# Turned FFN input projection: all 512-column products of a contraction half, then all 256-column ones

## The chip, the cores and the metric

The kernel runs on one core of a Trainium2 chip, in one launch. The core has five engines with queues of their own: TensorE (PE: matmuls, with its weight loads listed as PEld), VectorE (DVE), ScalarE (ACT), GpSimd (POOL) and SyncE (SP, which issues most of the DMAs). TensorE adds its products up in PSUM, of which the kernel uses eight banks of 128 partitions x 512 floats; everything else lies in SBUF. The metric is the device time of one execution in microseconds, as the median over several runs.

## The reference

Two layers of a streaming encoder on 256 tokens of width 1024, all in 32-bit floats. Each layer has a half-step FFN, a mixer (differential attention beside an mLSTM) and a second half-step FFN, each between a norm before and a norm after. The change lies in the FFN alone, which runs four times (two layers, two each):

```python
D_MODEL, SEQ, DEPTH, D_FF = 1024, 256, 2, 2816

def _swiglu(h, w_in, w_out):
    gate, up = jnp.split(h @ w_in, 2, axis=-1)
    return (jax.nn.silu(gate) * up) @ w_out

h = _swiglu(_rmsnorm(x, g[0]), ffn_w_in[l, 0], ffn_w_out[l, 0])
x = x + 0.5 * _rmsnorm(h, g[1])
```

So per FFN 256 tokens are multiplied with a 1024 x 5632 matrix, gate and up are combined, and the result is multiplied with a 2816 x 1024 matrix.

## The kernel before

**Three products for one.** TensorE multiplies in a reduced format (float32r). To keep precision, each operand is split into a high part, rounded to that format, and a low part, what is left of it. A product is then high x high + high x low + low x high. The weights are split on the chip: `begin_piece` (line 276) loads a piece of 128 x 2048 floats (1 MB) by a DMA on SyncE into a tile `wr`; for each half of it ScalarE makes the high part `wh` (line 287) and VectorE the low part `wl` (line 288). The split takes 324 instructions of each kind.

**Chunks.** The 2816 hidden columns are cut into 11 chunks of 256 (`NC_FF`). A chunk needs three pieces of weights: two of the input matrix, one for each half of the contraction of 1024 (`kh` 0 and 1), and one of the output matrix. The loop over chunks is in `ffn` (line 588, loop from line 661). The first two chunks of a pass are computed token-major, `in_piece` with `mm3` (lines 400 to 402).

**Turned chunks.** From chunk 2 (`TURN`) on, nine chunks to a pass, the projection is turned: the weights are the stationary operand and the tokens move, so that the hidden block comes out with hidden columns on partitions. `in_turned` (line 603) computes a chunk for one half of the contraction. There are four blocks of 128 output columns, two for gate and up (`i`) times two (`j`), each with a PSUM bank of its own: `banks[0]` are two banks with the tag `pin`, `banks[1]` two with the tag `ptr`. For each block and each of four slices of the contraction (`k`) there are two matmuls:

- line 610: the high part of the weights, against `both`, where the high parts of all 256 tokens stand beside their low parts: 512 columns, high x high in the left half of the bank and high x low in the right half;
- line 613: the low part of the weights, against the high parts of the tokens alone: 256 columns, added to the left half of the bank.

The order before is block by block: four of line 610, four of line 613, then the next block. It is called twice, for `kh` 0 and 1, and both halves add up in the same banks.

**Evacuation.** `ffn_turned` and `ffn_block` (lines 575 and 561) take two banks per `j`: ScalarE copies the right half of a bank to SBUF (line 567), VectorE adds the left half to it (line 568; then the bank is free) and scales by token (line 569); ScalarE takes the SiLU of the gate (line 571, recorded at line 265), VectorE multiplies by the up part (line 572). `ffn_hilo` splits the hidden block for the output product (lines 545 and 546).

**Output product.** `out_part` (line 597) multiplies a hidden block with the output weights: 24 matmuls of 512 columns for a chunk, in four banks `bk`. It runs two chunks behind (`DEFER`). So the ordinary chunk on TensorE is: 32 matmuls of `kh` 0, 32 of `kh` 1, 24 of the output product of an earlier chunk. The last three output products of a pass come at its end, the first token half first (lines 689 to 697).

**What sets the order.** The engines' queues are in order. A planner places the instructions by priority and by readiness in a plan of its own; so TensorE's order can differ from the order in the source, except for the end of a pass (from "ending") and the first chunk, where the source's order is kept. Tiles and banks come from pools with a fixed number of buffers, and a write waits until the buffer's last reader is done.

Of the kernel before, what the change touches and what calls it, by code (L numbers as in the profile page):

```python
# [24 lines left out]
P = 128  # L25
D = 1024
S = 256
NT = S // P
# [102 lines left out]
class _Trunk:  # L131
# [456 lines left out]
    def ffn(self, pre, gi_post):  # L588
# [13 lines left out]

        def in_turned(banks, w, kh, both):

            for j in range(2):
                for i in range(2):
                    c = slice(i * 256 + j * P, i * 256 + j * P + P)
                    b = banks[j][i]
                    for k in range(4):
                        self.nc.tensor.matmul(b, self.cols(w, k)[0][:, c], both[:, k].rearrange("p i t -> p (i t)"),  # L610
                                              start=kh == 0 and k == 0, stop=False, skip_group_check=True)
                    for k in range(4):
                        self.nc.tensor.matmul(b[:, 0:NT * P], self.cols(w, k)[1][:, c], both[:, k, 0:NT].rearrange("p i t -> p (i t)"),  # L613
                                              start=False, stop=kh == 1 and k == 3, skip_group_check=True)

        po, pend = None, []
        if not xT:
# [43 lines left out]
        for c in range(begin, NC_FF):  # L661
            ws = [self.piece(), self.piece()]
            pend.append((c - 1, h, self.piece()))
            if c == 3:
                g = self.load_gpost(gi_post)
                yield "middle"
            if c < TURN:
                pins = [self.bank_pin() for _ in range(NT)]
                for kh in range(2):
                    for t in range(NT):  # L670
                        in_piece(t, kh, pins[t], ws[kh])
                h = [self.ffn_evac(pins[t], r[t]) for t in range(NT)]
            else:
                if c == TURN:
                    rows, both = self.token_scales(r), list(self.both)
                banks = [[self.bank_pin() for _ in range(2)], [self.bank_tr() for _ in range(2)]]
                for kh in range(2):
                    in_turned(banks, ws[kh], kh, both[kh])
                if c == NC_FF - 1:
                    break  # L680
                h = self.ffn_turned(banks, rows, c > NC_FF - DEFER - 1)
            if len(pend) == DEFER - 1 or po is None:
                if po is None:
                    po = [[self.bank_bk() for _ in range(2)] for _ in range(NT)]
                cc, hc, wo = pend.pop(0)
                for t in range(NT):
                    out_part(cc, t, hc, wo)
# [567 lines left out]
```

## Time and profile before

| | us |
|---|---|
| runs shown (three) | 977.34, 977.02, 977.38; median 977.34 |
| the profiled execution, time | 978.05 |
| its span, first to last instruction | 976.3 |
| TensorE busy in it | 968.3 |
| TensorE weight loads | 817.2 |
| VectorE busy | 710.5 |
| ScalarE busy | 567.5 |

The span is shorter than the execution's time, since what lies ahead of the first instruction and behind the last one isn't in it. Busy time counts the time in which an engine had an instruction under way; for TensorE, whose matmuls overlap, it says little of how well the array is used, and the distance from one start to the next says more. In the views below, "out<-in" are the program's tiles with buffer numbers left out (`pin<-both,wh`: into a bank `pin`, from `both` and `wh`), "128*128 128x512" is the stationary operand and the moving operand of a matmul, "x4" the number of instructions that were merged into the row, and a bracket tells the idle time ahead of a row and what ended it.

### The profile page before, as it was taken

How to read it: one execution, taken by the hardware profiler on the slowest of the kernel's cores; microseconds unless marked ns; L12 is line 12 of the kernel's file. 1: busy time of each engine (PE TensorE's matmuls, PEld its weight loads, DVE VectorE, ACT ScalarE, POOL GpSimd, SP SyncE). 2: the span in 40 equal slices, each digit the busy share in tenths (PEclk: the TensorE clock that was granted, in tenths of full speed). 3: DMA queues.
4: the chain of work that ended last, by engine and by line, in shares of the span. 5: the costliest groups of instructions: out<-in, count | busy, mean ns of one | idle time of the engine just before them, and what ended most of it. 6: DMA issues, size and time to landing. Idle time of an engine off the chain costs nothing.

```text
span 976.3 us, 13528 instructions
## 1 busy us (share of the span) xinstructions
PE 968.3 (99%) x5067; PEld 817.2 (84%) x5067; DVE 710.5 (73%) x1177; ACT 567.5 (58%) x1041; POOL 29.0 (3%) x55
## 2 busy tenths in 40 slices
PE   9999999999999999999999999999999999999997
PEld 6888888888788888888888888888888888888886
DVE  6787676689867677667687767676997687776764
ACT  7665555477856565455475545454778475555541
POOL 2000000000010000000000000000001000000000
PEclk9999999999999999999999999999999999999999
DMA  8864545336352844564356455443454256644511
GB/s 305 335 224 167 198 170 205 134 130 232 115 193 95 315 170 175 186 238 177 133 203 241 149 206 216 175 170 116 171 211 173 87 208 239 215 176 177 198 61 44
DMA packets 27648, 178.94 MB, mean 183 GB/s; under 512 B 3034, under 2 KB 4186, under 8 KB 6846
## 3 DMA queue, kind: packets, MB, share of 16 engines
q1 hardware_dynamic: 27006, 177.46, 49.5%
q8 instruction: 40, 0.66, 0.3%
q10 hardware_dynamic: 576, 0.61, 0.2%
q14 instruction: 26, 0.21, 0.1%
HBM read 177.01 MB, written 1.05 MB: 182 GB/s over the span
## 4 chain that ended last, share of the span: by engine, by line
PE 99%; DMA 1%; DVE 0%; SPq 0%; ACT 0%; POOLq 0%; issue 0%; DVEq 0%; ACTq 0%
PE ptr L610 14%; PE pin L610 14%; PE bk L402 10%; PE bk L401 10%; PE bk L400 10%; PE pin L400 7%; PE pin L402 7%; PE pin L401 7%; PE ptr L613 7%; PE pin L613 7%; PE ptr L877 1%; PE ptr L426 1%; PE bk L1092 1%; PE bk L1130 1%; DMA x<-in_x_dram 1%; PE bk L378 0%
## 5 line engine op out<-in xcount | busy, mean ns | idle before, releaser
L288 DVE TENSOR_TENSOR wl<-wr,wh 128x1024 fp32r<-128x1024 f32 x324 | 388.6, 1222 | 127.2 <-ACT wh L287 125.2
L287 ACT ACTIVATE wh<-wr 128x1024 fp32r<-128x1024 f32 x324 | 332.2, 1053 | 121.1 <-PE ptr L610 55.9
L610 PE MATMUL pin<-both,wh 128*128 128x512 f32 x576 | 157.3, 394 | 0.0
L610 PE MATMUL ptr<-both,wh 128*128 128x512 f32 x576 | 157.0, 394 | 0.0
L401 PE MATMUL bk<-wl,hh 128*128 128x512 f32 x352 | 137.6, 391 | 0.0
L400 PE MATMUL bk<-wh,hh 128*128 128x512 f32 x352 | 137.4, 390 | 0.0
L402 PE MATMUL bk<-wh,hl 128*128 128x512 f32 x352 | 136.8, 391 | 0.0
L400 PE MATMUL pin<-wh,both 128*128 128x512 f32 x304 | 122.4, 404 | 0.0
L401 PE MATMUL pin<-wl,both 128*128 128x512 f32 x304 | 119.1, 392 | 0.0
L402 PE MATMUL pin<-wh,both 128*128 128x512 f32 x304 | 118.8, 391 | 0.0
L610 PEld LDWEIGHTS pin<-both,wh 128*128 128x128 f32 x576 | 100.6, 189 | 14.9
L610 PEld LDWEIGHTS ptr<-both,wh 128*128 128x128 f32 x576 | 98.8, 189 | 13.8
L613 PEld LDWEIGHTS ptr<-both,wl 128*128 128x128 f32 x576 | 88.3, 189 | 12.2
L613 PEld LDWEIGHTS pin<-both,wl 128*128 128x128 f32 x576 | 88.2, 189 | 11.7
L613 PE MATMUL pin<-both,wl 128*128 128x256 f32 x576 | 92.4, 281 | 0.0
L613 PE MATMUL ptr<-both,wl 128*128 128x256 f32 x576 | 91.6, 281 | 0.0
L545 ACT ACTIVATE hh<-su 128x256 fp32r<-128x256 f32 (+1 forms) x96 | 32.1, 355 | 95.4 <-PE bk L401 79.1
L402 PEld LDWEIGHTS bk<-wh,hl 128*128 128x128 f32 x352 | 66.1, 188 | 14.0
L401 PEld LDWEIGHTS bk<-wl,hh 128*128 128x128 f32 x352 | 66.1, 188 | 12.9
L400 PEld LDWEIGHTS bk<-wh,hh 128*128 128x128 f32 x352 | 66.1, 188 | 12.8
L402 PEld LDWEIGHTS pin<-wh,both 128*128 128x128 f32 x304 | 57.1, 188 | 12.4
L400 PEld LDWEIGHTS pin<-wh,both 128*128 128x128 f32 x304 | 57.2, 188 | 11.8 <-issue 0.7
(202 smaller groups left out, 978.4 us busy)
## 6 DMA issues: line engine op xcount, KB each, us to landing
wr<-in_w_dram SPq DMA_DIRECT2D x162, 1024.0 KB, 4.8
gpost<-in_gpost_dram SPq DMA_DIRECT2D x6, 512.0 KB, 5.7
wr<-in_w_dram SPq DMA_DIRECT2D x2, 512.0 KB, 6.9
wr<-in_w_dram SPq DMA_DIRECT2D x3, 256.0 KB, 5.1
x<-in_x_dram SPq DMA_DIRECT2D x3, 256.0 KB, 5.7
out_dram<-x SPq DMA_DIRECT2D x2, 256.0 KB, 2.4
x<-in_x_dram SPq DMA_DIRECT2D x2, 128.0 KB, 2.8
wr<-in_w_dram ACTq DMA_DIRECT2D x1, 256.0 KB, 3.7
```

What stands on the lines that cost most here:

```text
L287: ia = nc.scalar.activation(hi, raw[:, j], AF.Copy)
L288: iv = nc.vector.tensor_tensor(lo, raw[:, j], hi.bitcast(F32), op=ALU.subtract)
L400: mm(ps, xh, wh, start=start, stop=False)
L401: mm(ps, xh, wl, start=False, stop=False)
L402: mm(ps, xl, wh, start=False, stop=stop)
L426: nc.tensor.transpose(ptr[:, k, :], x[:, (4 * hf + k) * P:(4 * hf + k + 1) * P], self.ident)
L545: self.nc.scalar.activation(hh, h, AF.Copy)
L610: self.nc.tensor.matmul(b, self.cols(w, k)[0][:, c], both[:, k].rearrange("p i t -> p (i t)"), start=kh == 0 and k == 0, stop=False, skip_ ...
L613: self.nc.tensor.matmul(b[:, 0:NT * P], self.cols(w, k)[1][:, c], both[:, k, 0:NT].rearrange("p i t -> p (i t)"), start=False, stop=kh == ...
L877: self.T(ptr[:, b, :], a[:, b * P:(b + 1) * P], self.tr.ident)
L1092: self.mm(pcs[c][:, h, :], self.qkT[0][rows, h0 + h, t * P:(t + 1) * P], self.qkT[1][rows, h0 + h, 0:nk], start=True, stop=True)
L1130: self.mm(po[:, h, :], self.aT[t][:, kt, h, :], self.vd[:, kt, h * P:(h + 1) * P], start=kt == 0, stop=kt == t)
```

## The change

Within each half of the contraction, `in_turned` goes over the four blocks twice: first all sixteen products of 512 columns (four blocks times four slices, line 610 before), then all sixteen of 256 columns (line 613 before). The blocks, their banks, the operands, the number of matmuls, and which of them starts and which ends the sum in a bank stay the same.

```diff
         def in_turned(banks, w, kh, both):
 
-            for j in range(2):
-                for i in range(2):
-                    c = slice(i * 256 + j * P, i * 256 + j * P + P)
-                    b = banks[j][i]
-                    for k in range(4):
-                        self.nc.tensor.matmul(b, self.cols(w, k)[0][:, c], both[:, k].rearrange("p i t -> p (i t)"),
-                                              start=kh == 0 and k == 0, stop=False, skip_group_check=True)
-                    for k in range(4):
-                        self.nc.tensor.matmul(b[:, 0:NT * P], self.cols(w, k)[1][:, c], both[:, k, 0:NT].rearrange("p i t -> p (i t)"),
-                                              start=False, stop=kh == 1 and k == 3, skip_group_check=True)
+            blocks = [(banks[j][i], slice(i * 256 + j * P, i * 256 + j * P + P)) for j in range(2) for i in range(2)]
+            for b, c in blocks:
+                for k in range(4):
+                    self.nc.tensor.matmul(b, self.cols(w, k)[0][:, c], both[:, k].rearrange("p i t -> p (i t)"),
+                                          start=kh == 0 and k == 0, stop=False, skip_group_check=True)
+            for b, c in blocks:
+                for k in range(4):
+                    self.nc.tensor.matmul(b[:, 0:NT * P], self.cols(w, k)[1][:, c], both[:, k, 0:NT].rearrange("p i t -> p (i t)"),
+                                          start=False, stop=kh == 1 and k == 3, skip_group_check=True)
```

## The prediction

> **What bounds the kernel now.** I read the page first: its span, busy times, granted clock and the chain that ended last.
>
> ```profile
> span 976.3 us, 13528 instructions
> PE 968.3 (99%) x5067; PEld 817.2 (84%) x5067; DVE 710.5 (73%) x1177; ACT 567.5 (58%) x1041; POOL 29.0 (3%) x55
> PEclk9999999999999999999999999999999999999999
> PE 99%; DMA 1%; DVE 0%; SPq 0%; ACT 0%; POOLq 0%; issue 0%; DVEq 0%; ACTq 0%
> ```
>
> TensorE is 99% of the chain, its clock is at full speed in every slice, and no other engine holds more than 1% of the chain. A busy TensorE proves little by itself, since the ends of matmuls are modelled, so I looked next at what TensorE waits for (the list of waits, TensorE alone).
>
> ```profile
> PE bk L389 <- PEq L1245: 0.8, 1, 0.8
> PE ptr L348 <- DMA x<-in_x_dram: 0.5, 1, 0.5
> PE bk L376 <- ACT wh L366: 0.4, 1, 0.4
> ```
>
> That is the whole list: 1.7 us, all of it in the opening stage (lines 348, 376 and 389). Behind it TensorE never waits for weights, for a bank or for an evacuation. The time of this kernel is therefore the sum of the distances from one matmul's start to the next, and the change can act in two ways only: it alters those distances, or it makes a wait where there is none. How many matmuls are concerned is in the costliest groups (line, engine, operation, shapes, count, then busy time, mean duration in ns, idle time before).
>
> ```profile
> L288 DVE TENSOR_TENSOR wl<-wr,wh 128x1024 fp32r<-128x1024 f32 x324 | 388.6, 1222 | 127.2 <-ACT wh L287 125.2
> L287 ACT ACTIVATE wh<-wr 128x1024 fp32r<-128x1024 f32 x324 | 332.2, 1053 | 121.1 <-PE ptr L610 55.9
> L610 PE MATMUL pin<-both,wh 128*128 128x512 f32 x576 | 157.3, 394 | 0.0
> L610 PE MATMUL ptr<-both,wh 128*128 128x512 f32 x576 | 157.0, 394 | 0.0
> L613 PE MATMUL pin<-both,wl 128*128 128x256 f32 x576 | 92.4, 281 | 0.0
> L613 PE MATMUL ptr<-both,wl 128*128 128x256 f32 x576 | 91.6, 281 | 0.0
> ```
>
> There are 1152 products of 512 columns and 1152 of 256, 32 of each to a chunk, so 36 turned chunks (9 in each of four FFN passes). Their durations of 394 and 281 ns overlap, so they are no prices. The price is the distance of starts, and the timeline gives it. This is one ordinary chunk, with the last ten output matmuls ahead of it (start, length, engine, line, shapes, count):
>
> ```profile
> 112.63 0.39 PE L402 MATMUL bk<-wh,hl 128*128 128x512 f32 x1
> ...
> 114.90 1.07 PE L610 MATMUL pin<-both,wh 128*128 128x512 f32 x4
> 115.81 0.64 PE L613 MATMUL pin<-both,wl 128*128 128x256 f32 x4
> 116.28 1.09 PE L610 MATMUL pin<-both,wh 128*128 128x512 f32 x4
> 117.21 0.63 PE L613 MATMUL pin<-both,wl 128*128 128x256 f32 x4
> 117.68 1.09 PE L610 MATMUL ptr<-both,wh 128*128 128x512 f32 x4
> ...
> 126.10 0.40 PE L400 MATMUL bk<-wh,hh 128*128 128x512 f32 x1
> ```
>
> The ten output matmuls, all of 512 columns, take 114.90 - 112.63 = 2.27 us, 0.227 each. The first four turned products of 512 columns, right behind them, take 0.91, still 0.2275 each. After the first four of 256 columns (0.47), the next four of 512 take 0.93, 0.2325 each. The same instruction costs about 5 ns more after a run of short ones. The whole chunk takes 126.10 - 114.90 = 11.20 us.
>
> **The change part by part.** No instruction is added or removed: the same 2304 matmuls with the same weight loads, the same banks, the same DMAs. What changes is the order within each half of the contraction: four long runs of four and four short ones become one of sixteen each. So I need the price of long runs. The planner has made a few in the first chunks of a pass, where it took blocks out of turn:
>
> ```profile
> 339.48 1.09 PE L610 MATMUL pin<-both,wh 128*128 128x512 f32 x4
> 340.41 1.07 PE L610 MATMUL ptr<-both,wh 128*128 128x512 f32 x4
> 341.31 0.64 PE L613 MATMUL ptr<-both,wl 128*128 128x256 f32 x4
> ...
> 345.52 0.63 PE L613 MATMUL ptr<-both,wl 128*128 128x256 f32 x4
> 345.99 0.64 PE L613 MATMUL pin<-both,wl 128*128 128x256 f32 x4
> 346.47 1.09 PE L610 MATMUL pin<-both,wh 128*128 128x512 f32 x4
> ...
> 353.00 0.28 PE L613 MATMUL ptr<-both,wl 128*128 128x256 f32 x1
> 353.11 1.09 PE L610 MATMUL ptr<-both,wh 128*128 128x512 f32 x4
> 354.04 0.99 PE L613 MATMUL ptr<-both,wl 128*128 128x256 f32 x7
> 354.87 1.09 PE L610 MATMUL ptr<-both,wh 128*128 128x512 f32 x4
> ```
>
> Step 1, the long products. In a run of eight the first four take 0.93 and the next four 0.90, so the extra is paid once at the return from short products, about 0.02 us in all, and the pace is then 0.227 again or a little under. A run of sixteen costs 16 x 0.227 = 3.63, plus 0.02 where it follows short ones. In each chunk the first half follows output matmuls (no extra), the second follows short products (extra).
>
> Step 2, the short products. A run of eight takes 0.95 (0.119 each) and a run of seven 0.83 (0.1186 each); a run of four is 0.47 to 0.48. Length does not matter here: sixteen cost 4 x 0.475 = 1.90.
>
> Step 3, the sum. First half 3.63 + 1.90 = 5.53, second half 5.55, together 11.08 us against 11.20. The timeline is rounded to 0.01 us and the return extra to about that much, so the gain is 0.11 to 0.13 per chunk; over 36 chunks 4.0 to 4.7 us. I take 4.4.
>
> The bounds: if a long product keeps 0.2325 in a run of sixteen, the gain is zero. On the other side stands the single short product at 353.00, behind long ones, which took 0.11; if all sixteen kept that, 1152 x 0.009 = 10 us more would go. Against this speak the four at 115.81, which follow the ten output matmuls shown and four long turned products and still take 0.47. I take the long-run rows, since they show the very sequence that the change makes.
>
> One rule of the Trainium skill speaks against any gain. Its page "TensorE: Matmul & The Clock Gate", section "Back-to-back issue gap", gives an isolated distance of N / 2.4 ns plus 2.5 ns, 216 ns for 512 columns and 109 for 256, set by a matmul's own width and not by its neighbours; as an estimate by that page a chunk of 32 and 32 would take 10.4 us in either order. The rows differ, 0.227 and 0.119 in runs, and show the neighbour's effect (0.91 and 0.93 for the same four).
>
> Step 4, the weights. The low parts (wl, line 288) are now first needed sixteen long products later, the high parts (wh, line 287) at the same moment; and wh is read for the last time 1.9 us sooner in its half, so ScalarE, which idles 55.9 us waiting for line 610 to let go of it, can convert sooner. TensorE waits for neither today, so this is worth nothing, and it costs nothing: both act away from a wait. The load queue of SyncE issues the same transfers, at most a little earlier.
>
> Step 5, the evacuation. This is where cover is spent. Today the four banks are finished one block apart, so VectorE works on the first while TensorE fills the others; then they are all finished within the last 1.9 us of the chunk. The rows of VectorE and ScalarE around one chunk's end, and the next chunk's claim on the last bank:
>
> ```profile
> 156.55 0.42 DVE L568 TENSOR_TENSOR su<-pin,su 128x256 f32<-128x256 f32 x1
> ...
> 159.89 2.36 DVE L288 TENSOR_TENSOR wl<-wr,wh 128x1024 fp32r<-128x1024 f32 x2 [0.32 <-ACT wh L287]
> 162.17 0.42 DVE L568 TENSOR_TENSOR su<-ptr,su 128x256 f32<-128x256 f32 x1
> ...
> 160.72 0.36 ACT L567 ACTIVATE su<-ptr 128x256 f32<-128x256 f32 x1
> ...
> 169.15 1.09 PE L610 MATMUL ptr<-both,wh 128*128 128x512 f32 x4
> ```
>
> Today the last bank is free at 162.17 + 0.42 = 162.59 and wanted at 169.15: 6.6 us of cover. After the change, by my working: this chunk's short products run from about 157.45 to 159.35; the first bank is full at 157.9, its copy (about 0.4) is done at 158.4. From there VectorE has four adds, four scalings and two products (10 x 0.43 = 4.3 us) and the pair of splits (2.36); less the 0.9 behind the last add, the last bank is free at about 164.2. The next chunk starts 5.5 us after 159.35, at 164.85, and its last bank comes after twelve long products (2.7), at 167.6. Cover 3.4 us: less than before, but enough, and the first bank (free near 159, wanted at 164.85) has more. Cost: nothing.
>
> Step 6, the end of a pass, where the hidden block is needed soonest:
>
> ```profile
> 180.71 0.29 DVE L546 TENSOR_TENSOR hl<-su,hh 128x128 fp32r<-128x128 f32 x1 [0.38 <-ACT hh L545]
> ...
> 182.33 0.39 PE L400 MATMUL bk<-wh,hh 128*128 128x512 f32 x1
> ```
>
> The second block's low part is ready at 181.00 and its first use stands at 182.33: 1.3 us. Bunching can push that chain by roughly two 0.42 us operations, 0.8 us, which still fits. If the planner puts more ahead of it, up to a split of 1.22 us, the wait is about 0.7 us, in four passes 3 us. I take nothing and keep 0 to 3 us for the range.
>
> The sum is made against the profiled execution: span 976.3, about 971.9 after. That execution took 978.05 us, 1.75 outside its span; the runs shown have their median at 977.34, so the forecast is 977.34 - 4.4 = 972.9.
>
> **The rivals.**
>
> A, no effect: each shape has one pace whatever runs beside it, or the planner, which places TensorE's instructions by readiness in its own plan, breaks the long runs up again (the single at 353.00 shows that it does this), so the order on the chip is hardly changed. For it: the difference of 5 ns is seen on few long runs. Against it: the 0.91 and 0.93 come back in every chunk, and what the planner takes out of turn lies in the first two chunks of a pass. If only those two of nine keep their old pace, 4.4 x 7 / 9 = 3.4 us is left, 973.9, inside the forecast. If all do: 977.3. The rule of the Trainium skill named above ("TensorE: Matmul & The Clock Gate", "Back-to-back issue gap") would have A come out.
>
> B, slower: the last bank becomes late. All four banks finish together, and VectorE's strict sequence puts weight splits in front of the last add. The point that decides is 3.4 us of cover, not quite three splits of 1.22 us beyond the pair already counted. With three, 3.66 - 3.4 = 0.26 us would be lost at each of 32 following chunks, 8 us: 972.9 + 8 = 981. Each further split adds up to 39 us. For it: VectorE is busy 73% of the time and handles six splits per chunk. Against it: today it has one pair in that stretch, and idled 0.32 us before it.
>
> C, more gain: a run of short products behind sixteen long ones stays at 0.11: 962 to 963. Against it, the 0.47 at 115.81.
>
> **How the numbers follow.** Forecast (971.0 to 974.5, with or without the first chunks and part of step 6) 0.68; A at about 977.3, or a mixture of it and waits at the ends of passes between 975.4 and 977.6, 0.21; B 0.08; C 0.03. The range goes from 970.8 to 977.6, which takes in the forecast and A and leaves out B and C. About 0.2%, 2 us, is what a measurement of this kernel tells from no change: faster than 975.4 has 0.68 + 0.03, and 0.01 from mixtures, 0.72; within 0.2% 0.20; slower 0.08.
>
> **What would show it.** In the timeline of the changed kernel an ordinary chunk should show 610 x16 lasting 3.63 to 3.66 from start to next start and 613 x16 lasting about 1.90, over four banks each, and the chunk 11.08. If the first group takes 3.72, A is right about the pace. If runs of four or mixed runs remain, the planner undid it. If the list of waits of TensorE names line 568 or 567 ahead of 610, B holds; if it names 545 or 546 ahead of 400, step 6 was underpriced. The forecast is wrong if short products in long runs cost more than 0.119, since nothing longer than eight is shown today: each ns more there costs 1.15 us.

## The result, and the profile after

The changed kernel is slower. Five executions took 984.25, 980.76, 984.0, 983.99 and 984.42 us (median 984.0), five of the kernel before 977.02 to 977.92 (median 977.38): a ratio of 1.0064, interval 1.0053 to 1.0075. The forecast was 972.9 with a range up to 977.6.

The page of the changed kernel, in the lines that were read first before:

```profile
span 982.4 us, 13506 instructions
PE 970.6 (99%) x5067; PEld 820.1 (83%) x5067; DVE 693.4 (71%) x1177; ACT 564.0 (57%) x1041; POOL 29.2 (3%) x55
PEclk9999999999999999999999999999999999999999
PE 98%; DVE 1%; ACT 1%; issue 0%; POOLq 0%; DVEq 0%; ACTq 0%
```

Little is to be seen here: a busy share of 99% again, and a clock that looks full in every slice of 24 us. The one hint is that VectorE and ScalarE have entered the chain that ended last, with 1% each. The list of what TensorE waits for (total, times, longest) tells more:

```profile
PE bk L400 <- ACT hh L545: 4.8, 3, 2.2
PE bk L389 <- PEq L1244: 0.8, 1, 0.8
```

A new line stands on top: three waits of the output product (line 400) for the high part of the hidden block (line 545). The timeline has the first of them at the end of the first FFN pass, TensorE alone (the bracket is the idle time ahead and what ended it):

```profile
179.98 0.39 PE L402 MATMUL bk<-wh,hl 128*128 128x512 f32 x1
182.58 0.50 PE L400 MATMUL bk<-wh,hh 128*128 128x512 f32 x1 [2.21 <-ACT hh L545]
182.92 0.59 PE L401 MATMUL bk<-wl,hh 128*128 128x512 f32 x1
183.30 0.63 PE L402 MATMUL bk<-wh,hl 128*128 128x512 f32 x1
183.73 0.63 PE L400 MATMUL bk<-wh,hh 128*128 128x512 f32 x1
```

From one start to the next 2.60 us go by where 0.227 is usual. And behind the wait the matmuls are slow: 0.34, 0.38 and 0.43 from start to start. The 0.34 of the first is not the clock's doing: behind a short wait at full clock the first takes 0.34 too (180.94 to 181.28 in the run below that has the new order in the last chunk alone). Stretches cut to these places (window, its length, PE busy and so on, then the granted clock) show why the others are slow:

```profile
179.98:182.58 2.60, 0.39 (x3) 0.01 (x1) 2.56 (x9) 0.78 (x3) 0.00 (x0) 1.00 0.88 350
182.58:186.56 3.98, 3.98 (x10) 3.15 (x11) 1.46 (x5) 1.23 (x5) 0.00 (x0) 0.57 0.70 290
182.95:186.36 3.41, 3.41 (x10) 2.67 (x9) 0.89 (x4) 0.86 (x3) 0.00 (x0) 0.50 0.72 300
479.33:481.93 2.60, 0.39 (x2) 0.00 (x0) 2.56 (x9) 0.78 (x3) 0.00 (x0) 1.00 0.76 321
481.93:486.84 4.91, 4.91 (x15) 3.88 (x15) 1.57 (x5) 1.78 (x7) 0.00 (x0) 0.65 0.61 234
483.33:486.74 3.41, 3.41 (x10) 2.64 (x9) 0.69 (x1) 1.13 (x3) 0.00 (x0) 0.50 0.49 204
668.64:669.42 0.78, 0.40 (x3) 0.01 (x1) 0.72 (x3) 0.70 (x3) 0.00 (x0) 1.00 0.52 158
```

Behind the two long waits the granted clock is 0.57 and 0.65 on average, which is half clock, 0.50, for 3.41 us each time. Behind the second wait it begins only at 483.33, 1.4 us after the wait has ended. The ten matmuls of the stretch from 182.58 take 3.98 us in place of 2.27; in the stretch from 481.93 fourteen take 4.91 in place of 3.18 (the fifteenth that is counted starts at its very end). So the bill is: waits of 2.37 + 2.37 + 0.55 = 5.3 us, slow matmuls 1.7 + 1.7 = 3.4 us, nearly all of it half clock, together 8.7. The spans differ by 6.1, so some 2.6 us came back elsewhere: about 2.0 in the turned products, whose distances from start to start add up to 401.6 us here and 403.6 before, and most of the rest in the opening, where TensorE's waits were 1.7 us before and are 0.8 here.

What was expected of the order itself is there. An ordinary chunk of the changed kernel on TensorE:

```profile
100.29 1.98 PE L608 MATMUL pin<-both,wh 128*128 128x512 f32 x8
102.10 1.98 PE L608 MATMUL ptr<-both,wh 128*128 128x512 f32 x8
103.92 1.12 PE L612 MATMUL pin<-both,wl 128*128 128x256 f32 x8
104.87 1.12 PE L612 MATMUL ptr<-both,wl 128*128 128x256 f32 x8
105.83 2.00 PE L608 MATMUL pin<-both,wh 128*128 128x512 f32 x8
107.67 1.98 PE L608 MATMUL ptr<-both,wh 128*128 128x512 f32 x8
109.48 1.12 PE L612 MATMUL pin<-both,wl 128*128 128x256 f32 x8
110.44 1.12 PE L612 MATMUL ptr<-both,wl 128*128 128x256 f32 x8
111.40 0.40 PE L402 MATMUL bk<-wh,hl 128*128 128x512 f32 x1
```

The long products take 3.63 and 3.65 us, as forecast; the short ones 1.91 and 1.92, where 1.90 was forecast; the chunk 11.11 in place of 11.20.

Why does the hidden block come late? VectorE at the same place, changed kernel:

```profile
177.49 2.36 DVE L288 TENSOR_TENSOR wl<-wr,wh 128x1024 fp32r<-128x1024 f32 x2 [1.83 <-PE ptr L612]
179.77 0.42 DVE L568 TENSOR_TENSOR su<-pin,su 128x256 f32<-128x256 f32 x1
180.10 0.74 DVE L568 TENSOR_TENSOR su<-ptr,su 128x256 f32<-128x256 f32 x2
180.76 1.08 DVE L569 TENSOR_TENSOR su<-su,rows 128x256 f32<-128x256 f32 x3
181.76 0.75 DVE L572 TENSOR_TENSOR su<-su 128x256 f32<-128x256 f32 x2
```

Two things are to be seen. First, the last turned products end at 177.46, but VectorE first does two splits of weights (177.49 to 179.8) and only then three of the four adds. Those splits belong to the first pieces of the next phase, whose first product TensorE starts at 196.10. Before, one add was left behind such a pair; now it is three. The rows of the kernel before:

```profile
176.63 2.36 DVE L288 TENSOR_TENSOR wl<-wr,wh 128x1024 fp32r<-128x1024 f32 x2
178.91 0.42 DVE L568 TENSOR_TENSOR su<-ptr,su 128x256 f32<-128x256 f32 x1
```

Second, between the end of the turned products and the first use of the hidden block there were 24 output matmuls (176.16 to 181.65, 5.5 us of cover); now there are 12 (177.46 to 182.58, with the wait in them). The planner has put the other 12 ahead of the last chunk and earlier: between the late chunks of this pass stand 31, 31, 31, 27, 24 and 12 output matmuls, where each gap had 24, and 48 are left for the end of the first token half and the second up to the next phase's transposes, where 60 were. By these counts the 12 are the first output matmuls of the end of the pass: the source's order holds among the matmuls of the end, but does not keep them behind the last chunk.

### The profile page after: what moved, and what is told of

It reads as the page before. It is cut to its first block, busy times and chain, and to the rows that moved or that the text cites. A ratio compares the mean times of both kernels' runs of the same rounds, so it can differ in the third digit from the quotient of the medians.

```text
span 982.4 us, 13506 instructions
## 1 busy us (share of the span) xinstructions
PE 970.6 (99%) x5067; PEld 820.1 (83%) x5067; DVE 693.4 (71%) x1177; ACT 564.0 (57%) x1041; POOL 29.2 (3%) x55
## 3 DMA queue, kind: packets, MB, share of 16 engines
q1 hardware_dynamic: 27006, 177.46, 49.1%
## 4 chain that ended last, share of the span: by engine, by line
PE 98%; DVE 1%; ACT 1%; issue 0%; POOLq 0%; DVEq 0%; ACTq 0%
PE pin L608 14%; PE ptr L608 13%; PE bk L400 10%; PE bk L402 10%; PE bk L401 9%; PE pin L400 7%; PE pin L402 7%; PE pin L401 7%; PE ptr L612 7%; PE pin L612 7%; PE ptr L876 1%; PE ptr L426 1%; PE bk L1091 1%; PE bk L1129 1%; PE bk L378 0%; PE bk L389 0%
## 5 line engine op out<-in xcount | busy, mean ns | idle before, releaser
L608 PE MATMUL pin<-both,wh 128*128 128x512 f32 x576 | 149.0, 393 | 0.0
L608 PE MATMUL ptr<-both,wh 128*128 128x512 f32 x576 | 142.9, 390 | 0.0
L608 PEld LDWEIGHTS ptr<-both,wh 128*128 128x128 f32 x576 | 107.1, 188 | 22.1
L608 PEld LDWEIGHTS pin<-both,wh 128*128 128x128 f32 x576 | 103.5, 189 | 19.2 <-DVE su L568 1.1
L612 PEld LDWEIGHTS pin<-both,wl 128*128 128x128 f32 x576 | 82.1, 190 | 7.8
L612 PE MATMUL pin<-both,wl 128*128 128x256 f32 x576 | 84.9, 282 | 0.0
L612 PE MATMUL ptr<-both,wl 128*128 128x256 f32 x576 | 80.9, 283 | 0.0
L612 PEld LDWEIGHTS ptr<-both,wl 128*128 128x128 f32 x576 | 75.5, 192 | 1.5
L265 ACT ACTIVATE su<-su 128x256 f32<-128x256 f32 x72 | 29.1, 411 | 76.9 <-DVE su L569 76.8
```

Source lines behind the costliest of these rows:

```text
L265: i = self.nc.scalar.activation(*args, **kw)
```

## The experiments

Eight kernels, each timed beside the kernel before on the same chip (977.37 in the first group of four, 977.58 in the second). The first theory was that the new order of the last chunk makes the wait, at the place where nothing is left to cover it.

**Block order in the last chunk of each pass alone.** `in_turned` gets an argument for the order: "blocks" is that of the kernel before, "long" that of the change ("short", below, has the 256-column products first):

```diff
-                    in_turned(banks, ws[kh], kh, both[kh])
+                    in_turned(banks, ws[kh], kh, both[kh], "blocks" if c == NC_FF - 1 else "long")
```

> The last chunk of each pass goes back to block order, the other 32 turned chunks keep the new order. Theory E (the loss is a wait of TensorE at the end of a pass, and the half clock behind it): no wait for line 545 on TensorE, granted clock 1.00 there, and what the longer runs give is left: 975.6 us (975.0 to 976.3). Rival R (the new order itself costs, all along the pass): 982 us or more, since 32 of 36 chunks keep it.

978.05 us, ratio 1.0008 (0.9999 to 1.0016). Both theories missed. The waits shrink but don't go:

```profile
PE bk L400 <- ACT hh L545: 1.7, 2, 0.8
```

The last chunk is computed in the old order here, and still only 12 output matmuls stand between it and the first use; TensorE stands 1.1 us at the end of the first and of the second pass. So the missing output matmuls come from the order of the chunks ahead of the last one.

**The new order in the last chunk alone**, blocks elsewhere (the two words exchanged).

> Block order everywhere but in the last chunk of each pass, which has the new order. Theory E: the whole loss and nearly none of the gain: 985 us (983 to 990), with waits of 2 us and more for line 545 at the ends of the first two passes. Rival R: 977.4 + 6.6 / 9 = 978.1 us.

978.03 us, ratio 1.0005 (0.9996 to 1.0014). Here theory E fell outright, and the rival hit by luck: there are waits, but small ones (line 545: 0.4 us in all on two occasions, with 0.60 us from start to start in place of 0.227). VectorE has the splits ahead of all four adds, which is worse than in the changed kernel:

```profile
175.13 2.36 DVE L288 TENSOR_TENSOR wl<-wr,wh 128x1024 fp32r<-128x1024 f32 x2 [1.95 <-PE ptr L614]
177.41 0.75 DVE L568 TENSOR_TENSOR su<-pin,su 128x256 f32<-128x256 f32 x2
178.07 0.74 DVE L568 TENSOR_TENSOR su<-ptr,su 128x256 f32<-128x256 f32 x2
```

But all 24 output matmuls are still behind the last turned chunk, and 5.5 us of cover take nearly all of it. So neither the order of the last chunk nor the splits alone make the loss; it needs the lost cover too.

**The next phase's splits held back.** New order everywhere, and the second halves of the next phase's first two pieces are split only behind the last chunk's line 546 for the first tokens:

```diff
+                split = [self.ffn_hilo(h[:, t], *(v[:, j] for v in ops[t])) for t in range(NT)]
+                self.evac = split[:1]
...
-            self.turns = [[], [], [], [], last[:1], post] if ph else []
+            evac = self.evac if ph in (1, 3, 4) else []
+            self.turns = [[], evac, [], evac, last[:1], post] if ph else []
```

> New order everywhere; the second halves of the next phase's first two pieces are split only behind the first token half's line 546 of the last chunk. Theory S (VectorE reaches the last three adds late because splits of the next phase stand ahead of them): the waits shrink from 2.4, 2.4 and 0.5 us to under 0.5 each, the clock stays at 1.00, 975.5 us (974.8 to 976.8). Rival T (the four banks are finished too close to the end, whatever stands ahead): waits of 1 us and more stay, 980 us or more.

975.55 us, ratio 0.9981 (0.9972 to 0.999), as theory S had it: no wait of the output product is left, although the 12 matmuls are still missing. VectorE's part of the timeline:

```profile
177.43 0.42 DVE L569 TENSOR_TENSOR su<-pin,su 128x256 f32<-128x256 f32 x1 [1.46 <-ACT su L568]
177.97 0.42 DVE L569 TENSOR_TENSOR su<-ptr,su 128x256 f32<-128x256 f32 x1
178.65 0.41 DVE L569 TENSOR_TENSOR su<-ptr,su 128x256 f32<-128x256 f32 x1
...
182.25 2.36 DVE L288 TENSOR_TENSOR wl<-wr,wh 128x1024 fp32r<-128x1024 f32 x2 [0.65 <-ACT wh L287]
```

The adds (one line further down in this kernel, 569) follow the banks at once and the splits come behind.

**The waits filled.** Changed kernel with ten matmuls of zeros, added into an open bank, at the places of the two long waits:

```diff
+            if p is pend[-1] and gi_post in (0, 2):
+                for _ in range(10):
+                    self.nc.tensor.matmul(po[0][1], self.zero.broadcast_to([P, P]), self.zero.broadcast_to([P, 512]),
+                                          start=False, stop=False, skip_group_check=True)
```

> New order everywhere; ten matmuls of zeros (512 columns) are added into an open bank ahead of the last chunk's output product, at the end of the first and second pass, where TensorE waits 2.4 us. Theory C (a part of the loss is the clock, which drops because TensorE stands idle): the granted clock stays at 1.00 in those windows and about 1.9 us come back at each: 980.3 us (979.8 to 981.2), close to the one execution of the changed kernel that took 980.76 at a clock of 0.999. Rival (the clock's share is nothing): 984.0 us, or a little more if the ten outlast the wait.

981.14 us, ratio 1.0035 (1.0023 to 1.0048): 2.9 us less than the changed kernel, by adding work. The hidden block comes as late as before, but the clock holds:

```profile
180.00:183.00 3.00, 2.99 (x15) 1.24 (x13) 2.96 (x10) 0.83 (x4) 0.00 (x0) 1.00 0.93 303
183.00:187.00 4.00, 4.00 (x18) 3.31 (x19) 1.79 (x7) 1.87 (x7) 0.00 (x0) 1.00 0.71 297
```

So about 3 us of the loss is the half clock, and it comes from TensorE standing idle.

**The source's order on TensorE.** The second theory was that the planner's move of 12 output matmuls is the other half of the cause. From chunk 4 of each pass on, TensorE's instructions are kept in the order of the source:

```diff
+            if c == 4:
+                yield "ending"
...
-        yield "ending"
         pend.append((c, self.ffn_turned(banks, rows, True), self.piece()))
```

> New order, and TensorE's instructions kept in the order of the source from chunk 4 of each pass on, so that the planner can't move output products ahead: 60 output matmuls again follow the last turned product in place of 48. Theory D (the loss comes from the 12 output matmuls that the planner moved ahead, which had covered the last evacuation): waits for line 545 under 0.5 us each, full clock, runs of sixteen: 975.0 us (974.3 to 976.2). Rival T (the banks are really free too late, and the planner filled a true gap): waits for line 568 ahead of the long products in most of the 28 chunks, 0.3 us or more each: 983 us or more.

974.93 us, ratio 0.9974 (0.9964 to 0.9984): theory D. TensorE's waits there:

```profile
PE bk L389 <- PEq L1245: 0.8, 1, 0.8
PE ptr L348 <- DMA x<-in_x_dram: 0.5, 1, 0.5
PE bk L400 <- ACT hh L545: 0.4, 2, 0.2
PE bk L376 <- ACT wh L366: 0.4, 1, 0.4
```

No wait for line 568: with nothing moved ahead, the next chunk's banks were free in time on the chip in all 28 chunks. So no gap at these banks had to be filled; if the planner moved the 12 matmuls for such a gap, it was one of its plan alone, and why it moved them is not shown. The fixed order also leaves more runs whole: 56 runs of sixteen long products, where the changed kernel has 30.

**Both: the source's order and the splits held back.**

> As the one with the source's order, and the next phase's second halves split behind line 546 as in the hold run: what the order itself is worth with every wait taken away. With the distances measured in the changed kernel (0.227 for a long product, 0.023 us extra for a return, 0.113 for the first short one and 0.120 for the rest) a chunk takes 11.11 in place of 11.20 us, over 36 chunks 3.3 us: 974.2 us (973.6 to 975.2). If the prediction's sum of 4.4 us was right: 972.9. Rival T: 983 us or more.

974.13 us, ratio 0.9962 (0.9948 to 0.9976), and no wait for line 545. This is what the order itself is worth: 3.45 us. No run has the two cures with the block order, but the kernel before shows no wait behind the opening that they could take away; and from start to start the turned products take 3.0 us less than before and the output matmuls 0.4 less.

**Short products first in the second half.** The chunk then ends with sixteen long products, the banks are finished 0.9 us apart and the short products of both halves form one run of 32:

```diff
-                    in_turned(banks, ws[kh], kh, both[kh])
+                    in_turned(banks, ws[kh], kh, both[kh], "short" if kh else "long")
```

> In the first half of the contraction long products first, in the second half short ones first: the short ones of both halves stand together, one run of 32 to a chunk, the chunk ends with sixteen long products and the banks are finished 0.9 us apart. Theory D: the planner leaves 24 and 60 output matmuls where they were, no wait at the end of a pass; one return to long products per chunk in place of two (the output matmuls need none): 973.3 us (972.5 to 974.3). Rival (any order that finishes the banks in less time than block order loses the cover): waits for line 545 and 979 us or more.

973.39 us, ratio 0.9956 (0.9943 to 0.9968). It has neither the hold nor a fixed order, and the planner leaves 24 output matmuls in each ordinary gap and 60 at the end by itself. This beats both kernels.

**All three together.**

> Short products first in the second half, the source's order on TensorE from chunk 4 on, and the hold of the next phase's splits: all three together. Theory D: as the short-first run with a little less, 972.9 us (972.2 to 974.0), no wait for line 545. Rival (the hold or the fixed order costs something of its own): 0.5 us or more above the short-first run.

973.23 us, ratio 0.9953 (0.9941 to 0.9966): no wait behind the opening, and no more than 0.16 us from the run before, which these runs can't tell apart. Hold and fixed order cost nothing that can be seen here and are not needed with this order.

Four of the kernels make a table of two by two, all with the new order:

| | splits of the next phase ahead | held back |
|---|---|---|
| 12 output matmuls moved ahead | 984.0 (the change) | 975.55 |
| source's order, none moved | 974.93 | 974.13 |

Either cure alone takes nearly the whole loss away; only both faults together open the long waits and let the clock fall. The lower row differs in the whole runs too: of the 1.4 us between 975.55 and 974.13, about 1.0 lies in the distances of the turned products.

## Why the prediction was wrong

**Step 6 failed**, the end of a pass, where I took nothing and kept 0 to 3 us for the range. It moved the chain by two small operations of VectorE and took it for granted that the first use of the hidden block would stay where it was, 24 output matmuls behind the last turned product. The first use came 12 matmuls (2.7 us) sooner, and the pair of splits stood ahead of three adds in place of one. The waits alone were 5.3 us in three passes (the fourth has no next phase whose splits could be in the way, and has no wait). The sign to look for was named rightly, lines 545 or 546 ahead of 400; the price was not.

**Step 5 was right about the chip and blind to the planner.** It worked out that the banks would be free 3.4 us before the next chunk claims them, and the run with the source's order shows no such wait. Which bank has the least cover it had wrong, though: it let the splits fall among the adds, but in that run they stand ahead of all four, so the first bank comes free only at 128.26 and is wanted at 131.00, 2.7 us. And it closed with "Cost: nothing". The cover it saw shrinking is what the planner weighs too, and the planner answered by moving output matmuls ahead. That the chunks ahead of the last one do this is shown by the two runs that changed one or the other; that the planner took their banks for not yet free is argued from its rule, not shown. The prediction knew that the planner takes work out of turn, but used it only in rival A, for the length of runs.

**The half clock was not in the sum at all.** Step 6's bound of 3 us counted waits alone, and no row of the kernel before showed an idle TensorE behind the opening. The run with the filled waits prices it at 2.9 us.

**Steps 1 to 3, the order itself: right in mechanism, mis-sized.** The sum was 4.4 us, and with every wait gone it is 3.45. The mis-sized term is step 2: sixteen short products take 1.915 us, not 1.90, since in a long run they settle at 0.120 and only the first is quick, while each of the groups of four that step 2 multiplied has a quick first one of its own. Over 72 runs of sixteen that is 1.1 us, about the whole difference between 4.4 and 3.45. Long products were met, 3.63 and 3.65 against 3.63 and 3.65. The forecast per chunk was 11.08, measured 11.11 and, with every wait gone, 11.10. In the changed kernel itself less arrived, some 2.0 us, since the planner broke up more runs than the two first chunks of each pass that rival A allowed for.

**Rivals.** A (no effect) is out: the run with both cures is 3.45 us faster than before. The rule of the Trainium skill that stood beside it ("TensorE: Matmul & The Clock Gate", "Back-to-back issue gap") goes by a matmul's own width alone, for isolated matmuls; here the order alone moved the time by 0.4%. B was right that it would be slower, but for the wrong place: it looked for the wait at the next chunk's banks, and not at the output product that uses the hidden block. TensorE's matmuls have no such wait in their list, its weight loads a small one:

```profile
PEld pin L608 <- DVE su L568: 1.1, 4, 0.3
```

It stands ahead of the last chunk of each pass, where only 12 output matmuls are left as cover; in the first pass the four long products there take 1.03 us in place of 0.91. C is out: only the first short product of a run goes at 0.11.

## What to carry to other kernels

Where a planner or a scheduler places the instructions, a change of order in one place is also a change of what stands ahead and behind it elsewhere: ask not only whether the cover is enough, but whether the planner will spend it, and look first at the end of a loop, where nothing comes after to make up for it. An evacuation that is spread over the work stays cheap; if an order is to group like instructions, group them so that the results are still finished one after another (here: short products first in the second half). And a wait of TensorE is priced with the slow matmuls behind it, not by its own length.

## What the runs showed of the hardware

Matmuls of 512 columns in this format settle at 0.227 us from start to start, those of 256 at 0.120. The first short one behind long ones goes at 0.11, and the first four or five long ones behind short ones cost 0.02 to 0.03 us more in all, so the order of widths alone was worth 3.45 us in 977.

A pause of 2.60 us between two starts was enough to bring the granted clock to half for 3.41 us, beginning 0.4 us behind the one pause and 1.4 us behind the other; pauses of 0.6 to 1.3 us, in the runs that had them, cost no such stretch of half-speed matmuls. It doesn't happen each time: one execution of the changed kernel took 980.76 at a mean clock of 0.999, against 984 at 0.994 to 0.997 for the four others, the same 3 us as in the run with filled waits. The Trainium skill ("TensorE: Matmul & The Clock Gate", "What's actually happening") has the clock fall to half after about 3.4 us without work, counted in windows that run freely. Half speed agrees (0.43 us from 183.30 to 183.73, against 0.227); the pause that sufficed here was shorter than that window. The clock's own record agrees with fixed windows: the stretches at full clock in the changed kernel last 177.49, 296.96 and 491.52 us, which is 52, 87 and 144 times 3.413, and in the 3.41 us ahead of each half-clock stretch TensorE was busy for 1.20 and 1.39 us. The same page's account of windows that don't start with the kernel would fit that it happens in some executions only, which these runs don't settle.
